# Products for z and the first gate in steps between the q, k, v blocks, and weights loaded as half tiles

## The chip, the core and the metric

The kernel runs on one core of one Trainium2 chip. Five engines matter here: TensorE (PE in the profile, PEld for its weight loads), VectorE (DVE), ScalarE (ACT), GpSimd (POOL) and SyncE (SP, which issues most of the transfers). Each runs its own queue of instructions in a fixed order, and they wait for each other through semaphores. The metric is the device time of one execution in microseconds.

## The reference

One residual block over 256 tokens of 2048 channels, in fp32. Only its first part, the token mixers, is touched by the change:

```python
def hybrid_mixer(h, w_in, conv_qkv, a_log, dt_bias, gdn_norm, pool_w, pool_scale,
                 w_branch_a, w_branch_b, w_mix_out):
    qkv, z, b_raw, a_raw, p, gate_a, gate_b = jnp.split(h @ w_in, splits, axis=-1)
    qkv = jax.nn.silu(causal_dwconv(qkv, conv_qkv))
    q, k, v = jnp.split(qkv, [QK_W, 2 * QK_W], axis=-1)      # 16 heads of 128
    ...
    o = gated_delta_rule(q, k, v, g, beta)
    o = rms_norm(o, gdn_norm) * jax.nn.silu(z.reshape(B, S, GDN_HEADS, GDN_DV))
    y_a = o.reshape(B, S, V_W) @ w_branch_a
    y_b = multi_scale_pool(p, pool_w, pool_scale) @ w_branch_b
    merged = jax.nn.sigmoid(gate_a) * y_a + jax.nn.sigmoid(gate_b) * y_b
    return merged @ w_mix_out
```

`gated_delta_rule` works in chunks: per head it needs products of k with k and q, decays between positions, a triangular solve and a few products with the state. Behind the mixers follow a cross-attention (weights xk, xq, xv, xo) and a gated MLP (ua, ub, dn).

## The kernel before

Every fp32 weight is split in two parts of 12 bits, `whi` (cast on ACT, L154) and `wlo` (subtraction on DVE, L155), and so is each activation; a product takes three of the four partial products. Weights come from memory as `raw` tiles of 128 x 2048 (1024 KB, three buffers, L140 and L141) and are split in two halves of 1024 columns; `whi` and `wlo` have three buffers each. Both halves of a raw tile are split in one go, before the first matmul on them (`wchunk`).

There are two forms of dense product. `proj_cm` (L163) gives 128 channels by 256 tokens: 16 pairs of a matmul with `whi` over 512 columns (L171) and one with `wlo` over 256 (L174). q, k, v of a head, the beta and decay logits (ba) and the pooling input (p) take this form. `proj_tm` (L186) gives tokens by 512 channels for both token tiles; each half of weights holds two rows of 128 and makes 2 x 6 matmuls of 512 columns (L195 to L197). z, the two gates (ga, gb) and all other products take it. Each `proj` has its own PSUM buffers out of four (`ps_acc`, L75).

Small work is written as generators in two lanes, "a" and "b", and `tick()` (L126) advances each lane by one step, every four rows in `proj_cm` and after each token tile of a half in `proj_tm`. So the text of the program puts the small instructions between the pieces of the dense products. The list scheduler of the tile framework then fixes each engine's queue from this program order and from what it expects to be ready.

The 16 heads run in four groups (`gdn_group`, L534). A group is 12 blocks (q, k, v of four heads); `conv_silu` (L520) follows each: the copy `t` of one half of PSUM on ACT and the sum on DVE, the multiplication with the row factors R, the first tap `ca` on ACT, three taps on DVE, and a SiLU on ACT into KQ or `vc`. Lane "a" transposes the results (`kqT` with its squares and `ktok`, `vT` with the copy into V). Then come z of the group (L584) with a SiLU on each token tile, `drain("a")`, and `gdn_rest` (L593) is put in lane "b". Behind the group the gate ga of the same index follows (`sigm`, L857), during which lane "b" works off the beginning of `gdn_rest`: `sse` and `rinv` (DVE, POOL), eight scalings of V (VZ, L611), eight products `Ur` each on POOL and ACT (L622, L625), the matmuls `gap` (L629), Exp (L633), a mask on POOL, the matmuls `kq` (L641). The rest of `gdn_rest` goes on during the next group. In group 0 lane "b" also holds `decays`, a long chain of elementwise work on POOL, which ends with the transposes bgT (L504). After group 3 and ga come gb (four products) and p.

ACT holds one table of functions at a time: a SiLU, a sigmoid and an Exp each need their own, and an `ACT_TABLE_LOAD` stands in its queue at each switch.

Of the kernel before, what the change touches and what calls it, by code (L numbers as in the profile page):

```python
# [11 lines left out]
ALU = mybir.AluOpType  # L12
# [13 lines left out]
def kernel(  # L26
    ctx: ExitStack,
    tc: tile.TileContext,
    x: bass.AP,          # [256, 2048]
    x_cm: bass.AP,       # [2, 128, 8, 256]  x, channel-major  # L30
    mem_cm: bass.AP,     # [2, 128, 8, 256]
    w_cm: bass.AP,       # [57, 128, 2048]   (q,k,v per head; b/a; p), channel-major blocks
    w_z: bass.AP,        # [4, 128, 16, 512]
    w_ga: bass.AP,       # [4, 128, 16, 512]
    w_gb: bass.AP,       # [4, 128, 16, 512]
    w_ya: bass.AP,       # [4, 128, 16, 512]
    w_yb: bass.AP,       # [4, 128, 8, 512]
    w_mo: bass.AP,       # [4, 128, 16, 512]
    w_pool: bass.AP,     # [128, 2048]       (c | group, out block, in block, d)
    w_xq: bass.AP,       # [16, 128, 2048]  # L40
    w_xk: bass.AP,       # [16, 128, 2048]
    w_xv: bass.AP,       # [4, 128, 16, 512]
    w_xo: bass.AP,       # [4, 128, 16, 512]
    w_up: bass.AP,       # [86, 128, 2048]
    w_dn: bass.AP,       # [4, 128, 43, 512]
    conv_w: bass.AP,     # [128, 48, 4]
    ffn_w: bass.AP,      # [128, 86, 3]
    ffn_b: bass.AP,      # [128, 86]
    pregain: bass.AP,    # [128, 4, 16]      (mix, xa, mem, ffn)
    postgain: bass.AP,   # [3, 128, 2048]  # L50
    gdn_gain: bass.AP,   # [128, 1]
    pool_sc: bass.AP,    # [128, 8]
    ab: bass.AP,         # [16, 2]           (a_log, dt_bias)
    c_ident: bass.AP,    # [128, 128]
    c_le: bass.AP,       # [128, 128]        1 where partition <= column
    c_gt: bass.AP,       # [128, 128]        1 where partition > column
    c_tinit: bass.AP,    # [128, 256]
    c_invc: bass.AP,     # [128, 64]
    out: bass.AP,        # [256, 2048]
# [15 lines left out]
    def ps_acc(name):  # L75
        return acc.tile([P, 512], F32, tag="acc", name=name)
# [4 lines left out]
    # ------------------------------------------------------------ constants  # L81
# [5 lines left out]
    # x channel-major first: its products begin before the norm is known  # L87
# [27 lines left out]
    # ------------------------------------------------------------ lanes of small work,  # L115
    # emitted a step at a time between the pieces of the dense products
# [21 lines left out]
    # ------------------------------------------------------------ weights  # L138
    def wraw(src, n, name):
# [4 lines left out]
    def wchunk(src, n, name, raw=None, keep=False):  # L144
        """Load n columns of weights and split them exactly in two parts of 12 bits."""
        raw = wraw(src, n, name) if raw is None else raw
        return list(wsplit(raw, n, name, keep))

    def wsplit(raw, n, name, keep=False):
        for s in range(0, n, 1024):  # L150
            m = min(1024, n - s)
            hi = wp.tile([P, 1024], F32R, tag="whi", name=f"whi_{name}_{s}")
            lo = wp.tile([P, 1024], F32R, tag="wlo", name=f"wlo_{name}_{s}")
            pin(nc.scalar.copy(hi[:, :m], raw[:, s:s + m]), keep)  # L154
            pin(nc.vector.tensor_tensor(out=lo[:, :m], in0=raw[:, s:s + m],  # L155
                                        in1=hi[:, :m].bitcast(F32), op=ALU.subtract), keep)
            yield hi, lo, m
# [5 lines left out]
    def proj_cm(wsrc, X, name, raw=None, parts=None):  # L163
        """out^T block [128 channels, 256 tokens]: product of the high weights with
        both parts of X side by side, of the low weights with the high part."""
        ps = ps_acc(f"cm_{name}")
        kt = 0
        for hi, lo, m in parts or wchunk(wsrc, 2048, name, raw):
            for j in range(m // P):
                xk = X(kt)  # L170
                nc.tensor.matmul(ps, lhsT=hi[:, j * P:(j + 1) * P],  # L171
                                 rhs=xk.rearrange("p a s -> p (a s)"),
                                 start=(kt == 0), stop=False)
                nc.tensor.matmul(ps[:, 0:S], lhsT=lo[:, j * P:(j + 1) * P],  # L174
                                 rhs=xk[:, 0, :], start=False, stop=(kt == 15))
                kt += 1
                if kt % 4 == 0:
                    tick()
        return ps
# [6 lines left out]
    def proj_tm(wsrc, X, KT, name, tail=0, mid=None):  # L186
        """out [128 tokens, 512] for both token tiles; over the last 2 * tail rows of
        128 the first token tile goes first, and mid(its product) follows it."""
        ps = [ps_acc(f"tm{t}_{name}") for t in range(NT)]
# [9 lines left out]
        def chunks(k0, k1):  # L199
            for c0 in range(k0, k1, 4):  # L200
                n = min(4, k1 - c0)
                src = wsrc[:, c0:c0 + n, :].rearrange("p k c -> p (k c)")
                kt = c0
                for hi, lo, m in wchunk(src, n * 512, f"{name}_{c0}"):
                    yield [(kt + j, hi[:, j * 512:(j + 1) * 512], lo[:, j * 512:(j + 1) * 512])
                           for j in range(m // 512)]
                    kt += m // 512

        K0 = KT - 2 * tail
        for part in chunks(0, K0):  # L210
            for t in range(NT):
                for args in part:
                    mm(t, *args)
                tick()
        if tail:
            parts = list(chunks(K0, KT))
            for t in range(NT):
                for part in parts:
                    for args in part:
# [4 lines left out]
        return ps  # L224

    # ------------------------------------------------------------ activations
# [11 lines left out]
    def transpose_in(dst, src, gain, name):  # L238
        """src(t) [128 tokens, 512] -> dst [128, 4, 2, 256] with the gain of each channel."""
# [20 lines left out]
    def rstd_of(parts, name, tag="rstd", bufs=8):  # L260
        """(sum of the columns / 2048 + eps) ** -0.5; parts: [128, n] sums of squares."""
# [11 lines left out]
    def square_sum(src, dst, name):  # L273
        """dst [128, 1] = sum of src ** 2 over [128, 512]."""
# [3 lines left out]
    def pre_norm(src, gi, name, tiles, ss):  # L278
        """src: two [128, 2048] tiles, scaled in place; appends the transposed tiles."""
# [13 lines left out]
    def row_factors(ss, name, first=False):  # L293
        """[128, 256]: on each partition the factors of the tokens."""
# [15 lines left out]
    def cm_squares(src, name, keep=False):  # L310
        """The sums of squares of the tokens, from channel-major tiles."""
# [23 lines left out]
    def result(gen):  # L335
        while True:
            try:
                next(gen)
            except StopIteration as e:
                return e.value  # L340

# [4 lines left out]
    def norm_cm(src, R, gi, name, tiles):  # L346
        """src: channel-major tiles, normalised in place and split."""
# [57 lines left out]
    # ============================================================ 1. mixers  # L405
    raw_q = wp.tile([P, 2048], F32, tag="raw", name="raw_q0")
# [4 lines left out]
    def load_q(q):  # L411
        sl = slice(q * 1024, (q + 1) * 1024)
        nc.sync.dma_start(raw_q[:, sl], w_cm[0][:, sl])
# [7 lines left out]
    # without the factor of each token, for the first blocks  # L421
    uT = []
    qparts = []
    qsplit = wsplit(raw_q, 2048, "q0", True)
    for b in range(4):
# [9 lines left out]
        if b % 2 == 0:  # L435
            qparts.append(next(qsplit))
    raw_k = wraw(w_cm[1], 2048, "k0")
    conv_sb = cload("conv_sb", conv_w, [P, 48, 4], nc.sync)
    raw_v = wraw(w_cm[2], 2048, "v0")
    raw_ba = wraw(w_cm[48], 2048, "ba")  # L440
# [14 lines left out]
    # beta and the log decays, channel-major: b in rows 0..15, a in rows 32..47  # L455
# [3 lines left out]
    # eG[:, 0, c, h] = exp(G_i), eG[:, 1, c, h] = exp(G_last - G_i)  # L459
# [5 lines left out]
    def decays(ps):  # L465
# [17 lines left out]
        # log(1 + e) = 2 atanh(e / (2 + e))  # L483
# [50 lines left out]
    def gdn_group(gi):  # L534
# [30 lines left out]

        for hl in range(4):
            h = 4 * gi + hl
            n = f"{g_}_{hl}"
            if h == 1:
                lanes["b"].append(decays(proj_cm(w_cm[48], U0, "ba", raw_ba)))  # L570
# [628 lines left out]
```

## Time and profile before

| what | value |
|---|---|
| time, median of 3 runs | 2026.81 us (2026.27 to 2026.9) |
| span of the profiled execution | 2026.0 us |
| PE busy | 2001.8 us, 99% of the span |
| DVE busy | 1386.6 us, 68% |
| ACT busy | 1099.6 us, 54% |
| POOL busy | 108.5 us, 5% |
| ACT table loads | 19, at 1.283 us |

The profiled execution has a time of its own, the span, from the first to the last instruction; the time of a run has a little around it. Busy shares are means over the whole program. The group stage, which the change touches, runs from the start to some 580 us: four groups of about 111 us (12 blocks, z and ga), then gb and p. A matmul's row overlaps the next one's by its fill, so the distance of two starts tells what one costs.

### The profile page before, as it was taken

The numbers are of one execution on the slowest core, as the hardware profiler recorded it, in microseconds if no ns is written. First come the engines' busy times: TensorE is split into PE (matmuls) and PEld (weight loads), VectorE is DVE, ScalarE is ACT, GpSimd is POOL, SyncE is SP. The second block draws the span as 40 slices with busy tenths as digits, with TensorE's granted clock in tenths as the row PEclk, the third lists the DMA queues.
The fourth block names the chain that finished last, engine by engine and source line by source line (L and its number), as shares of the span: only waits on it lengthen the run. The fifth ranks groups of instructions, "written<-read, shape, count | busy, mean of one in ns | idle before, by whom it ended". The sixth has DMA issues, their size and how long they took to land.

```text
span 2026.0 us, 27927 instructions
## 1 busy us (share of the span) xinstructions
PE 2001.8 (99%) x10842; PEld 1703.1 (84%) x10842; DVE 1386.6 (68%) x2171; ACT 1099.6 (54%) x1826; POOL 108.5 (5%) x154
## 2 busy tenths in 40 slices
PE   8999999999999999999999999999999999999998
PEld 6888888888878888888888888788888888888886
DVE  7869687697756855678555554688888887854444
ACT  7657666566654544456444444565555555544443
POOL 1510200201100000001000000100000000000000
PEclk9999999999999999999999999999999999999999
DMA  6445354444444656456555455555555555565553
GB/s 242 166 167 183 132 184 147 160 173 146 166 170 153 236 193 249 173 199 228 185 190 175 159 207 190 204 209 187 190 189 192 193 193 187 187 231 200 188 196 141
DMA packets 55029, 377.87 MB, mean 187 GB/s; under 512 B 6768, under 2 KB 7536, under 8 KB 10224
## 3 DMA queue, kind: packets, MB, share of 16 engines
q1 hardware_dynamic: 52128, 359.73, 51.0%
q0 software_dynamic: 2192, 15.73, 2.0%
q8 instruction: 85, 1.39, 0.3%
q10 hardware_dynamic: 576, 0.62, 0.1%
q14 instruction: 48, 0.39, 0.1%
HBM read 369.77 MB, written 6.29 MB: 186 GB/s over the span
## 4 chain that ended last, share of the span: by engine, by line
PE 95%; DVE 1%; POOL 0%; ACT 0%; issue 0%; DVEq 0%; POOLq 0%; ACTq 0%
PE cm_ub L171 8%; PE cm_ua L171 8%; PE cm_ub L174 4%; PE cm_ua L174 4%; PE tm_dn L197 4%; PE tm_dn L196 4%; PE tm_dn L195 4%; PE cm_xk L171 3%; PE cm_xq L171 3%; PE cm_vg L171 3%; PE cm_kg L171 2%; PE cm_qg L171 2%; PE tm_gb L195 2%; PE cm_xk L174 1%; PE cm_xq L174 1%; PE tm_gb L196 1%
## 5 line engine op out<-in xcount | busy, mean ns | idle before, releaser
L171 PE MATMUL cm_ua<-h3T,whi_ua 128*128 128x512 f32 x688 | 242.0, 395 | 0.0
L171 PE MATMUL cm_ub<-h3T,whi_ub 128*128 128x512 f32 x688 | 241.0, 394 | 0.0
L174 PE MATMUL cm_ua<-h3T,wlo_ua 128*128 128x256 f32 x688 | 191.0, 278 | 0.0
L174 PE MATMUL cm_ub<-h3T,wlo_ub 128*128 128x256 f32 x688 | 190.7, 277 | 0.1
L155 DVE TENSOR_TENSOR wlo_dn<-raw_dn,whi_dn 128x1024 fp32r<-128x1024 f32 (+1 forms) x88 | 105.6, 1200 | 119.0 <-ACT whi_dn L154 118.8
L154 ACT CAST whi_dn<-raw_dn 128x1024 fp32r<-128x1024 f32 (+1 forms) x88 | 91.1, 1035 | 136.9 <-PE tm_dn L197 132.2
L171 PEld LDWEIGHTS cm_ua<-h3T,whi_ua 128*128 128x128 f32 x688 | 129.3, 188 | 29.8 <-ACT h3T L253 0.2
L171 PEld LDWEIGHTS cm_ub<-h3T,whi_ub 128*128 128x128 f32 x688 | 129.1, 188 | 29.9
L155 DVE TENSOR_TENSOR wlo_ub<-raw_ub,whi_ub 128x1024 fp32r<-128x1024 f32 x86 | 105.3, 1225 | 58.1 <-ACT whi_ub L154 58.0
L154 ACT CAST whi_ub<-raw_ub 128x1024 fp32r<-128x1024 f32 x86 | 90.4, 1051 | 100.3 <-issue 51.5
L154 ACT CAST whi_ua<-raw_ua 128x1024 fp32r<-128x1024 f32 x86 | 90.6, 1053 | 99.2 <-PE cm_ub L171 47.5
L195 PE MATMUL tm_dn<-whi_dn,gT 128*128 128x512 f32 x344 | 133.8, 389 | 0.0
L196 PE MATMUL tm_dn<-wlo_dn,gT 128*128 128x512 f32 x344 | 133.8, 389 | 0.0
L197 PE MATMUL tm_dn<-whi_dn,gT 128*128 128x512 f32 x344 | 133.8, 389 | 0.0
L174 PEld LDWEIGHTS cm_ub<-h3T,wlo_ub 128*128 128x128 f32 x688 | 129.2, 188 | 0.4 <-DVE wlo_ub L155 0.4
L174 PEld LDWEIGHTS cm_ua<-h3T,wlo_ua 128*128 128x128 f32 x688 | 129.5, 188 | 0.0
L155 DVE TENSOR_TENSOR wlo_ua<-raw_ua,whi_ua 128x1024 fp32r<-128x1024 f32 x86 | 105.3, 1225 | 26.6 <-ACT whi_ua L154 26.5
L171 PE MATMUL cm_vg<-uT,whi_vg 128*128 128x512 f32 x256 | 95.1, 409 | 0.0
L171 PE MATMUL cm_kg<-uT,whi_kg 128*128 128x512 f32 x256 | 93.7, 406 | 0.0
L171 PE MATMUL cm_xk<-meT,whi_xk 128*128 128x512 f32 x256 | 89.7, 396 | 0.0
L171 PE MATMUL cm_xq<-h2T,whi_xq 128*128 128x512 f32 x256 | 88.8, 394 | 0.0
L171 PE MATMUL cm_qg<-uT,whi_qg 128*128 128x512 f32 x240 | 86.4, 401 | 0.0
(412 smaller groups left out, 5350.2 us busy)
## 6 DMA issues: line engine op xcount, KB each, us to landing
raw_ua<-in_w_up_dram SPq DMA_DIRECT2D x43, 1024.0 KB, 4.8
raw_ub<-in_w_up_dram SPq DMA_DIRECT2D x43, 1024.0 KB, 4.8
raw_dn<-in_w_dn_dram SPq DMA_DIRECT2D x40, 1024.0 KB, 4.7
raw_zg<-in_w_z_dram SPq DMA_DIRECT2D x16, 1024.0 KB, 4.8
raw_ga<-in_w_ga_dram SPq DMA_DIRECT2D x16, 1024.0 KB, 4.8
raw_gb<-in_w_gb_dram SPq DMA_DIRECT2D x16, 1024.0 KB, 4.7
raw_ya<-in_w_ya_dram SPq DMA_DIRECT2D x16, 1024.0 KB, 4.8
raw_mo<-in_w_mo_dram SPq DMA_DIRECT2D x16, 1024.0 KB, 4.7
```

The source lines that it names most:

```text
L154: pin(nc.scalar.copy(hi[:, :m], raw[:, s:s + m]), keep)
L155: pin(nc.vector.tensor_tensor(out=lo[:, :m], in0=raw[:, s:s + m], in1=hi[:, :m].bitcast(F32), op=ALU.subtract), keep)
L171: nc.tensor.matmul(ps, lhsT=hi[:, j * P:(j + 1) * P], rhs=xk.rearrange("p a s -> p (a s)"), start=(kt == 0), stop=False)
L174: nc.tensor.matmul(ps[:, 0:S], lhsT=lo[:, j * P:(j + 1) * P], rhs=xk[:, 0, :], start=False, stop=(kt == 15))
L195: nc.tensor.matmul(ps[t], lhsT=xh, rhs=wh, start=(k == 0), stop=False)
L196: nc.tensor.matmul(ps[t], lhsT=xh, rhs=wl, start=False, stop=False)
L197: nc.tensor.matmul(ps[t], lhsT=xl, rhs=wh, start=False, stop=(k == KT - 1))
```

## The change

Raw tiles become half as large (1024 columns, 512 KB) and twice as many (six), and a half is split right before its first matmul. The four PSUM buffers become two pairs; the blocks of a group use pair A, z and ga pair B. z and ga of a group become one generator of 18 turns (`gdn_side`: eight halves of z, the SiLU, eight halves of ga, the gate), and `blk` runs one or two turns of it after each block, in group 0 after all but the first head's, so that the generator is at its end with the last v. `gdn_rest` is put in lane "b" at the end of the group, and the next group's q block (after group 3: gb) follows at once. The ba weights are no longer loaded ahead. Comments are stripped, so line numbers move by up to 30.

```diff
+    def ps_acc(name, pair=None):
+        if pair is None:
+            pair = "AB"[acc_n[0] // 2 % 2]
+            acc_n[0] += 1
+        return acc.tile([P, 512], F32, tag=f"acc{pair}", bufs=2, name=name)
...
-        raw = wp.tile([P, 2048], F32, tag="raw", name=f"raw_{name}")
-        nc.sync.dma_start(raw[:, :n], src)
+        raw = wp.tile([P, 1024], F32, tag="raw", bufs=6, name=f"raw_{name}")
+        nc.sync.dma_start(raw[:, :src.shape[1]], src)
...
+    def proj_cm(wsrc, X, name, raws=None, parts=None, pair=None):
+        ps = ps_acc(f"cm_{name}", pair)
+        if parts is None and raws is None:
+            raws = wraws(wsrc, name)
+        for kt in range(16):
+            if kt % 8 == 0:
+                hi, lo = parts[kt // 8] if parts else wsplit(raws[kt // 8], f"{name}_{kt}")
...
+    def tm_steps(wsrc, X, KT, name, tail=0, mid=None, pair=None):
...
+        for k in range(0, K0, 2):
+            p = part(k, min(k + 2, K0))
             for t in range(NT):
-                for args in part:
+                for args in p:
                     mm(t, *args)
                 tick()
+            yield
...
+        side = gdn_side(gi, g_, zs)
+        turn = [0, 0]
+        N = 9 if gi == 0 else 12
+
+        def blk(*args):
+            ps = proj_cm(*args, pair="A")
+            turn[0] += 1
+            while turn[1] * N < 18 * turn[0]:
+                next(side, None)
+                turn[1] += 1
+            return ps
...
-            psq = proj_cm(w_cm[3 * h], U0, f"q{n}", parts=qparts if h == 0 else None)
-            psk = proj_cm(w_cm[3 * h + 1], U0, f"k{n}", raw_k if h == 0 else None)
+                psq = blk(w_cm[3 * h], U0, f"q{n}")
+                psk = blk(w_cm[3 * h + 1], U0, f"k{n}")
...
-        ps = proj_tm(w_z[gi], U0, 16, f"z{g_}")
-        for t in range(NT):
-            nc.scalar.activation(zs[:, t, :], ps[t], AF.Silu,
-                                 scale=R0[1][t][:, 0:1])
+        for _ in side:
+            pass
         if gi == 0:
             drain("b")
         drain("a")
         lanes["b"].append(gdn_rest(gi, g_, KQ, V, zs, ktok, ss))
 
+    def gdn_side(gi, g_, zs):
+        ps = yield from tm_steps(w_z[gi], U0, 16, f"z{g_}", pair="B")
+        for t in range(NT):
+            nc.scalar.activation(zs[:, t, :], ps[t], AF.Silu,
+                                 scale=R0[1][t][:, 0:1])
+        yield
+        ps = yield from tm_steps(w_ga[gi], U0, 16, f"ga{gi}", pair="B")
+        gate(ps, mga[gi // 2][:, gi % 2])
...
     for gi in range(4):
-        gdn_group(gi)
         if gi % 2 == 0:
             mga.append(b8(f"mga{gi}").rearrange("p (n t s) -> p n t s", n=2, t=2))
-        sigm(w_ga[gi], mga[gi // 2][:, gi % 2], f"ga{gi}")
+        gdn_group(gi)
```

The order of the instructions at the end of group 1 shows what moves. In the rows a name carries its group and head (`vc_g1_3` is the fourth v of group 1, `whi_qg2_0_8` the second half of the first q block of group 2) and a number of its own at the end. First PE before, where the last `vT` of the group stands:

```order
L197 MATMUL tm1_zg1_2273<-whi_zg1_12_1024_2448,uT3_145 128x512
L562 MATMUL vT_g1_3_2476<-ident_82,vc_g1_3_2261 128x128 x2
L195 MATMUL tm0_ga1_2482<-whi_ga1_0_0_2486,uT0_110 128x512
L196 MATMUL tm0_ga1_2482<-wlo_ga1_0_0_2487,uT0_110 128x512
L197 MATMUL tm0_ga1_2482<-whi_ga1_0_0_2486,uT0_110 128x512
...
L629 MATMUL gap_g10_2527<-Ur_g1_2517,m_gtr_166 128x512 x2
L195 MATMUL tm1_ga1_2483<-whi_ga1_0_0_2486,uT0_110 128x512
```

The whole of z stands between the last v block and its transposes, and ga around what follows. The same place on PE now:

```order
L180 MATMUL cm_vg1_3_2627<-uT3_146,wlo_vg1_3_8_2653 128x256
L554 MATMUL kqT_g1_3_2685<-ident_82,KQ_g1_1331 128x128 x4
L178 MATMUL cm_qg2_0_2708<-uT0_111,whi_qg2_0_0_2713 128x512
...
L567 MATMUL vT_g1_3_2699<-ident_82,vc_g1_3_2674 128x128 x2
L661 MATMUL gap_g10_2752<-Ur_g1_2742,m_gtr_169 128x512 x2
L661 MATMUL gap_g11_2785<-Ur_g1_2742,m_gtr_169 128x512
L673 MATMUL kq_g10_2812<-KQ_g1_1331 128x256
L178 MATMUL cm_qg2_0_2708<-uT2_133,whi_qg2_0_8_2765 128x512
```

Only the first half of the next q block (16 matmuls) and `kqT` stand between the last v block and `vT`. On ACT, the queue at that place before:

```order
L154 CAST whi_ga1_0_1024_2490<-raw_ga1_0_2484 128x1024
L625 ACTIVATE Ur_g1_2517<-m_le_162,g_lo_182 128x128 x2
L586 ACTIVATE VZ_g1_1377<-tm0_zg1_2272,rstd_h0_285 128x512
L625 ACTIVATE Ur_g1_2517<-m_le_162,g_lo_182 128x128 x3
L563 COPY VZ_g1_1377<-vT_g1_3_2476 128x256
L586 ACTIVATE VZ_g1_1377<-tm1_zg1_2273,rstd_h1_291 128x512
L611 ACTIVATE VZ_g1_1377<-VZ_g1_1377,rinv_g1_2502 128x128 x2
L154 CAST whi_ga1_4_0_2565<-raw_ga1_4_2563 128x1024
L633 ACT_TABLE_LOAD
L633 ACTIVATE UD_g1_2518<-gap_g10_2527 128x512
L154 CAST whi_ga1_4_1024_2569<-raw_ga1_4_2563 128x1024
L633 ACTIVATE UD_g1_2518<-gap_g11_2552 128x512
```

A cast stands after every few small instructions, and there is one table load. The queue of ACT at that place now, from the sixth scaling on:

```order
L530 ACTIVATE ca_vg1_3_2679<-xp0_95,conv_sb_159 128x256
L643 ACTIVATE VZ_g1_1332<-VZ_g1_1332,rinv_g1_2727 128x128 x5
L657 ACTIVATE Ur_g1_2742<-m_le_165,g_lo_185 128x128
L537 ACT_TABLE_LOAD
L537 ACTIVATE vc_g1_3_2674<-ca_vg1_3_2679 128x256
L657 ACTIVATE Ur_g1_2742<-m_le_165,g_lo_185 128x128
L158 CAST whi_qg2_0_8_2765<-raw_qg2_0_1024_2711 128x1024
L568 COPY VZ_g1_1332<-vT_g1_3_2699 128x256
L665 ACT_TABLE_LOAD
L665 ACTIVATE UD_g1_2743<-gap_g10_2752 128x512
L643 ACTIVATE VZ_g1_1332<-VZ_g1_1332,rinv_g1_2727 128x128 x2
L657 ACTIVATE Ur_g1_2742<-m_le_165,g_lo_185 128x128 x4
```

Two table loads and the SiLU of `vc` now stand among the scalings, and one cast in this stretch; the next, `whi_zg2_0`, follows the last row.

## Rows read from the trace of the kernel before

**Rows 1.** Engine shares of the page: busy time, share of the span, instructions.

```profile
PE 2001.8 (99%) x10842; PEld 1703.1 (84%) x10842; DVE 1386.6 (68%) x2171; ACT 1099.6 (54%) x1826; POOL 108.5 (5%) x154
```

**Rows 2.** Waits of PE: for what, us in total, times, longest.

```profile
PE cm_qg L171 <- ACT whi_q L154: 8.4, 1, 8.4
PE bgT L504 <- POOL st L499: 1.7, 1, 1.7
PE cm_vg L174 <- DVE wlo_vg L155: 1.3, 1, 1.3
```

**Rows 3.** 50 us windows: PE, PEld, DVE, ACT, POOL busy, clock, DMA share, GB/s.

```profile
100.00:150.00 50.00, 50.00 (x230) 41.53 (x229) 30.30 (x57) 29.67 (x49) 5.77 (x6) 1.00 0.49 170
400.00:450.00 50.00, 50.00 (x276) 43.11 (x275) 46.92 (x115) 31.58 (x53) 2.88 (x3) 1.00 0.50 171
```

**Rows 4.** Windows of 3.41 us behind the bgT wait, same columns.

```profile
72.85:76.26 3.41, 3.41 (x14) 3.02 (x14) 2.24 (x5) 1.73 (x4) 0.00 (x0) 0.50 0.66 274
76.26:79.67 3.41, 3.41 (x21) 3.04 (x21) 3.04 (x6) 2.68 (x6) 2.47 (x4) 1.00 0.36 86
```

**Rows 5.** Groups of ACT, 85 to 125 us: count, busy us, mean ns, idle before.

```profile
L154 ACT CAST whi_zg<-raw_zg 128x1024 fp32r<-128x1024 f32 x8 | 8.4, 1048 | 8.2 <-PE tm_zg L197 4.1 <-PE cm_vg L171 2.2 <-issue 1.2
L532 ACT ACTIVATE vc_g<-ca_vg 128x256 f32<-128x256 f32 x2 | 0.8, 410 | 0.0
L525 ACT ACTIVATE ca_vg<-xp,conv_sb 128x256 f32<-128x256 f32 x1 | 0.5, 507 | 0.0
```

**Rows 6.** The same of DVE.

```profile
L155 DVE TENSOR_TENSOR wlo_zg<-raw_zg,whi_zg 128x1024 fp32r<-128x1024 f32 x8 | 9.8, 1224 | 8.1 <-ACT whi_zg L154 8.1
```

**Rows 7.** DMA issues: count, KB each, median us to landing.

```profile
raw_zg<-in_w_z_dram SPq DMA_DIRECT2D x16, 1024.0 KB, 4.8
raw_pool<-in_w_pool_dram SPq DMA_DIRECT2D x2, 512.0 KB, 3.7
```

**Rows 8.** Timeline of PE: start, us, line, out<-in.

```profile
93.91 0.40 PE L171 MATMUL cm_vg<-uT,whi_vg 128*128 128x512 f32 x1
94.27 0.40 PE L171 MATMUL cm_vg<-uT,whi_vg 128*128 128x512 f32 x1
...
116.15 0.38 PE L562 MATMUL vT_g<-ident,vc_g 128*128 128x128 f32 x2
116.28 0.48 PE L195 MATMUL tm_zg<-whi_zg,uT 128*128 128x512 f32 x1
...
119.12 0.39 PE L195 MATMUL tm_ga<-whi_ga,uT 128*128 128x512 f32 x1
...
126.82 1.02 PE L641 MATMUL kq_g<-KQ_g 128*128 128x256 f32 x4
127.50 0.58 PE L195 MATMUL tm_ga<-whi_ga,uT 128*128 128x512 f32 x1
```

**Rows 9.** Timeline of POOL, end of the chain of decays.

```profile
71.78 0.53 POOL L499 TENSOR_SCALAR st<-st,aexp 16x256 f32<-16x256 f32 x1
```

**Rows 10.** Timeline of ACT, 103 to 123 us.

```profile
103.38 0.42 ACT L532 ACTIVATE vc_g<-ca_vg 128x256 f32<-128x256 f32 x1
...
108.71 0.27 ACT L554 ACTIVATE j_g<-kqT_g 128x128 f32<-128x128 f32 x1
...
109.72 0.28 ACT L556 COPY ktok_g<-kqT_g 128x128 f32<-128x128 f32 x1
111.94 0.99 ACT L611 ACTIVATE VZ_g<-VZ_g,rinv_g 128x128 f32<-128x128 f32 x3 [1.94 <-POOL rinv_g L603]
...
119.90 1.04 ACT L154 CAST whi_ga<-raw_ga 128x1024 fp32r<-128x1024 f32 x1
120.96 1.28 ACT L633 ACT_TABLE_LOAD   x1
122.25 0.60 ACT L633 ACTIVATE UD_g<-gap_g 128x512 f32<-128x512 f32 x1
122.75 1.04 ACT L154 CAST whi_ga<-raw_ga 128x1024 fp32r<-128x1024 f32 x1
```

More of the change, by code (lines that the diff above doesn't have):

```diff
@@ L136, in drain, with wraw, wraws, wsplit @@
             step(lanes[k])
-    def wraw(src, n, name):
-        raw = wp.tile([P, 2048], F32, tag="raw", name=f"raw_{name}")
-        nc.sync.dma_start(raw[:, :n], src)
-        return raw
[L144 to L157, printed above, removed]
+    def wraw(src, name):
+        raw = wp.tile([P, 1024], F32, tag="raw", bufs=6, name=f"raw_{name}")
+        nc.sync.dma_start(raw[:, :src.shape[1]], src)
+        return raw
+    def wraws(src, name):
+        return [wraw(src[:, s:s + 1024], f"{name}_{s}") for s in range(0, src.shape[1], 1024)]
+    def wsplit(raw, name, n=1024, keep=False):
+        hi = wp.tile([P, 1024], F32R, tag="whi", name=f"whi_{name}")
+        lo = wp.tile([P, 1024], F32R, tag="wlo", name=f"wlo_{name}")
+        pin(nc.scalar.copy(hi[:, :n], raw[:, :n]), keep)
+        pin(nc.vector.tensor_tensor(out=lo[:, :n], in0=raw[:, :n],
+                                    in1=hi[:, :n].bitcast(F32), op=ALU.subtract), keep)
+        return hi, lo
     def pin(ins, keep=True):
@@ L161, in pin @@
             tc.keep_in_program_order(ins)
[L163 to L178, printed above, removed]
+    def proj_cm(wsrc, X, name, raws=None, parts=None, pair=None):
[5 more added lines that the diff above has]
+                hi, lo = parts[kt // 8] if parts else wsplit(raws[kt // 8], f"{name}_{kt}")
+            sl = slice(kt % 8 * P, (kt % 8 + 1) * P)
+            xk = X(kt)
+            nc.tensor.matmul(ps, lhsT=hi[:, sl], rhs=xk.rearrange("p a s -> p (a s)"),
+                             start=(kt == 0), stop=False)
+            nc.tensor.matmul(ps[:, 0:S], lhsT=lo[:, sl], rhs=xk[:, 0, :], start=False,
+                             stop=(kt == 15))
+            if kt % 4 == 3:
+                tick()
         return ps
@@ L224, in proj_tm, with result @@
         return ps
+    def result(gen):
+        while True:
+            try:
+                next(gen)
+            except StopIteration as e:
+                return e.value
+    def proj_tm(*args, **kw):
+        return result(tm_steps(*args, **kw))
     def xtile(name):
@@ L333, in cm_squares @@
         return [s2[:, t:t + 1] for t in range(NT)]
[L335 to L340, printed above, removed]
     def new_ss(name):
@@ L403, in piece @@
             return self.y[t][:, sl]
-    raw_q = wp.tile([P, 2048], F32, tag="raw", name="raw_q0")
+    raw_q = [wp.tile([P, 1024], F32, tag="raw", bufs=6, name=f"raw_q0{q}") for q in range(2)]
     def load_x(i, q):
@@ L435 @@
         if b % 2 == 0:
-            qparts.append(next(qsplit))
-    raw_k = wraw(w_cm[1], 2048, "k0")
+            qparts.append(wsplit(raw_q[b // 2], f"q0{b}", keep=True))
+    raw_k = wraws(w_cm[1], "k0")
     conv_sb = cload("conv_sb", conv_w, [P, 48, 4], nc.sync)
-    raw_v = wraw(w_cm[2], 2048, "v0")
-    raw_ba = wraw(w_cm[48], 2048, "ba")
+    raw_v = wraws(w_cm[2], "v0")
     m_le = cload("m_le", c_le, [P, P], nc.sync)
```

50 lines of the change are left out of this document (24 added, 26 removed).

## Prediction

> **What bounds the kernel now.** I read the shares of the engines first, then what TensorE (PE) waited for, then 50 us windows over the stage that the change touches, then the timelines at the end of one group. PE is busy 2001.8 of 2026.0 us, ScalarE (ACT) 54% of the span [rows 1]. The longest wait of PE, 8.4 us, is the start of the program, which the change leaves as it is [rows 2]. In the stage of the four groups the nine windows from 100 to 550 us all show PE busy 50.00 of 50; two stand here, and they leave 18 to 20 us of each free on ACT and 3 to 20 on VectorE (DVE) [rows 3]. What this stage can still give back is the wait for bgT (1.7 us) and one for a low half (1.3) [rows 2], and a stretch of half clock: right behind the bgT idle the granted clock was 0.50 for 3.41 us with 14 matmuls in it, and 1.00 in the next 3.41 us with 21 [rows 4], so between 3.41 x 7/21 = 1.1 and 3.41/2 = 1.7 us went there. That is at most 5 us, 0.25%. So the question is hardly what the change wins, but whether PE stays fed.
>
> PE is fed by a chain: the transfer of a half of weights, its cast on ACT (1.05 us) [rows 5], its subtraction on DVE (1.22 us) [rows 6], with three halves of run-ahead; all engines run their queues in a fixed order. A late instruction on ACT delays every cast behind it.
>
> **The change part by part.** *Same work.* Matmuls, casts and subtractions keep their numbers and shapes. From the gb products on only the small work of the last group moves; what follows, two thirds of the time, I cost at 0.
>
> *Half tiles.* A half now has its own transfer of 512 KB and six buffers; before, two halves shared one of 1024 KB in three: the same store. 1024 KB land in 4.8 us, 512 KB in 3.7 [rows 7]. A half is used up in 2.7 us (12 matmuls from 116.28 to 119.12, less 0.1 for the transposes ahead) [rows 8]; with six in flight there is 3.7 us of transfer against some 16 us of lead: 0. Only with one in flight at a time would it cost 3.7 - 2.7 = 1.0 us a half, and nothing forces that.
>
> *PSUM in pairs.* A q, k or v block has two buffers and not four, so the third block waits for the copy and sum of the first, about 0.4 us each at vc's shape [rows 5]. A step of z or ga, 2.7 us at the least, lies between: 0.
>
> *The bgT wait.* On ACT the new order puts one more table load (1.28) and a SiLU between the sigmoid and the exponential ahead of POOL's chain of polynomials, whose last link ended at 72.31 [rows 9]; so the chain starts about 1 us later, and on PE the bgT transposes come 0.6 us of work earlier. The wait grows from 1.7 to some 3.3: +1.6. Bounds: -1.7 (it vanishes) and +3. The small waits in front of it are swallowed by it: 0.
>
> *The ends of the groups.* This term decides. Before, PE had the eight halves of z behind the last v of a group, and then eight of ga: the last vc was ready at 103.8 us [rows 10] and its transposes came only at 116.15 [rows 8]; the squares, scalings and decays of gdn_rest lay beside some 40 us of dense products, whose casts need 1.05 of each 2.7 us of ACT. After, z and ga are used up when the last v ends, and the last vc and the start of gdn_rest stand in ACT's and PE's queues between the very next weights. I count ACT from the end of the last v of group 1 in the new order (PSUM copies at vc's 0.41 [rows 5]; scalings and the Ur, which have one shape, at 0.33; squares with ktok 1.29, from 108.71 to 110.00 [rows 10]). Rest of a cast 0.5, copy t 0.41, one Ur 0.33, squares and ktok 1.29: 2.5. Then ACT stands still for sse and rinv, 1.94 as before [rows 10]: 4.5. A scaling 0.33, ca 0.51, five scalings 1.65, Ur 0.33, table load 1.28, SiLU vc 0.41, Ur 0.33: 9.3. Only now comes the second half of the next q block: 10.4, its low half at 11.6. Copy of V 0.41, table load 1.28, Exp 0.60, two scalings and four Ur 1.98, cast whi_zg_0 1.05: 15.7; its low half 1.22: 16.9.
>
> PE's work up to the first use of that low half: kqT 0.4 (four transposes, at half of what two vT take, 0.2), the q block 16 x 0.36 = 5.7, vT 0.2, four gap matmuls at 0.225 = 0.9, three heads of kq at 0.85 (0.68 to the next start, 1.02 to the end) = 2.6, two z matmuls 0.46 [rows 8]: 10.3. PE loses 16.9 - 10.3 = 6.6; as ACT's short instructions overlap (the Exp at 122.25 ran 0.60, the next cast began at 122.75), I take 6.1. First PE sits at vT (3.3 us of work stand ahead of it, vc comes at 9.0), then at the low half of q, then at the one of z. The ends of groups 2 and 3 read the same, with gb for q after group 3: 3 x 6.1 = 18.3. At the end of group 0 the last step of ga follows v, and both q halves are cast by then: ACT goes t 0.41, table load, two sigmoids (at Exp's 0.60; the second waits for PE's 2.7): 3.3; ca, squares, ktok, two Ur: 5.8; table load, SiLU, eight scalings, copy of V, four Ur: 11.8; table load, Exp, two Ur, cast, subtraction: 16.6. PE has 2.7 + 0.4 + 5.7 + 0.2 + 0.9 + 3.4 + 0.46 = 13.8. Loss 2.8.
>
> Bounds of one end: 0, if a run-ahead of three halves (8.1 us) covers it; 9, if the heads of kq don't fill the waits.
>
> *Clock.* After 1.7 us of idle the clock was halved for 3.41 us, at a price of 1.1 to 1.7 [rows 4]. Each of the four ends has a stall as long; but part of a halved stretch will fall in the next wait. 1.0 each: 4.0, between 0 and 13.6 (two such stretches at each end, 1.7 apiece).
>
> *Table loads.* The order has 31 on ACT where it had 19. Those at the ends are in the sum above; the others, like the rest of the 12 x 1.28 = 15.4 us, have room in ACT's free time [rows 3]. In the trace a load starts right behind a cast (119.90 + 1.04; load at 120.96) and Exp follows at 122.25, so a switch costs 1.3 us [rows 10]. The Trainium skill (ScalarE: Activation LUTs, What ACT_TABLE_LOAD costs and Rules for kernel authors) speaks against this change: it advises to do all of one table set before switching, and gives about 2.7 us for a switch, load and drain together. The trace shows the load and no drain behind a cast; by the page's figure the nine loads at the ends would add some 1.4 each, an estimate of 12 us more, and the time would be 2066.
>
> Sum: 2.8 + 18.3 + 4.0 + 1.6 = 26.7. The profiled execution spans 2026.0 us, the runs took 2026.3 to 2026.9, median 2026.8, so 0.8 lies around the span: 2026.0 + 26.7 + 0.8 = 2053.5. **Forecast: 2054 us, 1.3% slower.**
>
> **Rivals.** *Half hidden.* If ACT doesn't stand still for rinv at the ends (1.94 each) and the Ur there, which wait for nothing late, have run before v ends (seven x 0.33 = 2.3), each end loses about 2, and the clock less: 2026.8 + 4 x 2 + 2 = 2037. For it: ACT has 18 us of 50 free ahead of the end [rows 3]. Against: in the new order the Ur stand behind the squares, and a queue passes nothing.
>
> *No stall, and the bgT wait won.* It decides at the end of a group: if the run-ahead of three halves (8.1) is longer than what ACT does ahead of the second q half (10.4), PE never waits; that is short by 2.3 only. If PE then also comes to bgT after POOL's chain, 1.7 and the half clock of 1.1 to 1.7 come back, and 2026.8 - 3.2 = 2023.6, at best 2021.5 with the low half's wait. For it: ACT's free time again. Against: vT stands in PE's order ahead of the second q half, and its vc comes at 9.0.
>
> *Deeper.* PE works the 10 to 14 us of each end at half clock for the most part, since one stall follows the other: 4 x 5 in place of 4.0, so 2070; with 9 lost at each end 2080. Against: the one halved stretch in the groups lasted 3.41 us [rows 4].
>
> That the products are not interleaved after all is excluded by the order.
>
> **How the numbers follow.** Forecast 0.62 (2040 to 2068), half hidden 0.14 (2031 to 2040), no stall 0.13 (2021 to 2031), deeper 0.11 (2068 to 2085). Since the trace has no drain, 0.02 of the forecast's 0.62 is for the page's dearer switch, within the same bounds. What can be told from no change is 0.2%, 4 us: of the no-stall case 0.04 lies below 2022.8 and 0.09 within; the rest, 0.87, is slower. The range leaves out about a tenth on either side: 2029 to 2072.
>
> **What would show it.** Right: the 50 us windows that hold the ends of groups (near 138, 250, 360 and 475 us) fall to 43 to 48 of PE, with clock under 1.00; PE waits there at vT, whi_qg, wlo_qg, wlo_zg and wlo_gb, 2 to 5 us at a time; bgT waits 3 us; ACT has 15 us more; the time from gb on is that of before. Wrong: PE stays at 50.00 in these windows; waits for raw tiles appear behind the casts (then the half tiles matter); or the waits are spread over all blocks and not gathered at the four ends (PSUM pairs, or late casts everywhere).

## The result, and the profile after

The changed kernel took 2061.2 us (2059.65 to 2062.12) against 2026.7: 34.5 us more, a ratio of 1.0167 with a 95% interval of 1.0154 to 1.018. The forecast was 2054, slower. The span of the profiled execution is 2060.4 us against 2026.0.

Where the time went is bounded first by a tile that both kernels have behind the touched stage, the products ya with the branch weights. The row of after gives number, duration in ns (least, median, most), first and last start:

```profile
L201 PE MATMUL tm_ya<-whi_ya,oT_g x128: 387/389/476, 722.8 to 848.4; 128*128 128x512 f32 x128
```

The first ya matmul starts at 722.8; in the kernel before it was 688.7. So 34.1 of the 34.4 us are lost in the mixers, and the rest of the program runs as before. Two windows, of before and then of after, split them (columns of [rows 3]):

```profile
0.00:688.70 688.70, 675.90 (x3962) 572.17 (x3963) 508.34 (x973) 428.76 (x856) 86.52 (x115) 1.00 0.49 169
0.00:722.80 722.80, 689.59 (x3963) 578.13 (x3964) 510.16 (x973) 444.87 (x868) 92.74 (x115) 0.98 0.54 163
```

For the same matmuls PE stood idle 20.4 us longer (33.2 for 12.8) and was busy 13.7 us longer. The engine shares of after, and its waits of PE of a us or more in the mixers, but for the one at the start of the program (7.9, before 8.4), in the columns of [rows 1, 2]:

```profile
PE 2015.5 (98%) x10842; PEld 1708.8 (83%) x10842; DVE 1388.9 (67%) x2171; ACT 1115.0 (54%) x1838; POOL 114.7 (6%) x154
```

```profile
PE vT_g L567 <- ACT vc_g L537: 10.5, 3, 4.0
PE bgT L509 <- POOL st L504: 4.6, 1, 4.6
PE cm_qg L178 <- ACT whi_qg L158: 2.4, 2, 1.2
PE kq_g L673 <- ACT UD_g L665: 2.0, 1, 2.0
PE cm_qg L180 <- DVE wlo_qg L159: 1.5, 2, 0.8
PE tm_zg L201 <- ACT whi_zg L158: 1.3, 1, 1.3
PE tm_gb L202 <- DVE wlo_gb L159: 1.2, 2, 0.8
PE tm_gb L201 <- ACT whi_gb L158: 1.2, 1, 1.2
```

The bgT wait of [rows 2] has grown from 1.7 to 4.6 us, and the other rows are new. The vT, qg, kq, whi_gb and one of the wlo_gb waits lie at the ends of groups, as these 50 us windows show (columns of [rows 3]):

```profile
150.00:200.00 50.00, 47.96 (x235) 39.85 (x234) 42.20 (x104) 32.12 (x59) 3.18 (x4) 0.97 0.53 159
250.00:300.00 50.00, 44.15 (x235) 37.47 (x234) 30.55 (x63) 34.85 (x82) 14.17 (x14) 0.93 0.36 105
400.00:450.00 50.00, 45.44 (x227) 38.00 (x226) 30.98 (x59) 34.27 (x70) 13.15 (x13) 0.93 0.43 133
550.00:600.00 50.00, 44.10 (x196) 35.87 (x195) 31.18 (x64) 36.34 (x64) 11.49 (x13) 0.93 0.45 137
```

The window from 100 to 150 us, which holds no end, is as full as in [rows 3] (PE busy 50.00, clock 1.00); those that hold an end of a group lost 2 to 6 us of PE's 50, and their granted clock is 0.93 to 0.97. The waits at the ends begin near 152, 280, 420 and 560 us. That is later than the prediction's 138, 250, 360 and 475: a group of the kernel before takes 131.5 us and not the 111 given ahead of the prediction (the q blocks of groups 1, 2 and 3 start at 145.4, 277.0 and 408.5), and what was given as the end of the stage, some 580 us, is 688.7. The stretches of half clock one by one, in the same columns (the first is at bgT, the others at the ends of groups 0, 1, 2, 2 and 3):

```profile
72.52:79.35 6.83, 6.46 (x18) 5.27 (x19) 1.90 (x4) 2.77 (x4) 5.56 (x9) 0.50 0.01 4
154.44:157.85 3.41, 3.41 (x8) 2.75 (x9) 2.33 (x5) 2.37 (x5) 0.91 (x2) 0.50 0.00 0
287.56:294.39 6.83, 5.48 (x15) 4.47 (x15) 1.93 (x3) 6.79 (x14) 0.64 (x1) 0.50 0.25 77
424.09:427.50 3.41, 2.94 (x10) 2.14 (x8) 1.46 (x4) 2.20 (x8) 2.08 (x2) 0.50 0.41 136
430.92:434.33 3.41, 3.41 (x10) 2.72 (x9) 1.75 (x3) 3.38 (x8) 0.64 (x1) 0.50 0.34 83
567.45:574.28 6.83, 4.97 (x14) 4.05 (x14) 1.57 (x3) 6.77 (x14) 1.63 (x3) 0.50 0.22 57
```

These are the answer to [rows 4], where there was one stretch of 3.41 us. I estimate that the work done in a halved stretch would have taken half as long (the pairs of q's matmuls start 0.64 us apart from 424.27 on, and 0.35 just before). PE's busy time in the five at the ends is 20.2 us, so some 10.1 went there; at bgT 3.2, where before had 1.7.

One end, that of group 1, first on ACT (start, us, line; idle time before in brackets) and then on PE:

```profile
273.65 1.28 ACT L881 ACT_TABLE_LOAD   x1
...
276.23 1.28 ACT L537 ACT_TABLE_LOAD   x1
...
277.96 1.28 ACT L881 ACT_TABLE_LOAD   x1
...
279.84 1.03 ACT L158 CAST whi_qg<-raw_qg 128x1024 fp32r<-128x1024 f32 x1
...
284.57 0.40 ACT L643 ACTIVATE VZ_g<-VZ_g,rinv_g 128x128 f32<-128x128 f32 x1 [1.64 <-POOL rinv_g L635]
...
287.15 1.28 ACT L537 ACT_TABLE_LOAD   x1
288.44 0.42 ACT L537 ACTIVATE vc_g<-ca_vg 128x256 f32<-128x256 f32 x1
...
289.06 1.03 ACT L158 CAST whi_qg<-raw_qg 128x1024 fp32r<-128x1024 f32 x1
...
293.91 1.03 ACT L158 CAST whi_zg<-raw_zg 128x1024 fp32r<-128x1024 f32 x1
```

```profile
280.92 0.50 PE L178 MATMUL cm_qg<-uT,whi_qg 128*128 128x512 f32 x1 [1.19 <-ACT whi_qg L158]
...
282.18 0.39 PE L180 MATMUL cm_qg<-uT,wlo_qg 128*128 128x256 f32 x1 [0.76 <-DVE wlo_qg L159]
...
288.91 0.69 PE L567 MATMUL vT_g<-ident,vc_g 128*128 128x128 f32 x2 [3.90 <-ACT vc_g L537]
```

The last v block of the group ended near 279.2 (the transposes kqT, 0.60 long, start at 279.14). Three table loads stand ahead of the cast of the next q's first half, which ends at 280.87; PE waits 1.19 for it and 0.76 for its low half. Then come the squares, the idle time for rinv (1.64, in [rows 10] 1.94), the scalings, a load, and the SiLU of vc, which ends at 288.86, 9.6 us behind the v block; PE waits 3.90. The second q half and whi_zg follow at 290.1 and 294.9, 10.9 and 15.7 behind the block.

The table loads on ACT by line, SiLU of q, k, v and sigmoid of the gates:

```profile
L537 ACT ACT_TABLE_LOAD x13 | 16.7, 1283 | 0.2
L881 ACT ACT_TABLE_LOAD x8 | 10.3, 1283 | 0.1
```

They were 5 and 4 before; in all 31 against 19.

### The profile page after: what moved, and what is told of

Read it like the earlier page. It is cut to its first block, busy times and chain, and to the rows that moved or that the text cites. A ratio compares the mean times of both kernels' runs of the same rounds, so it can differ in the third digit from the quotient of the medians.

```text
span 2060.4 us, 28816 instructions
## 1 busy us (share of the span) xinstructions
PE 2015.5 (98%) x10842; PEld 1708.8 (83%) x10842; DVE 1388.9 (67%) x2171; ACT 1115.0 (54%) x1838; POOL 114.7 (6%) x154
## 4 chain that ended last, share of the span: by engine, by line
PE 90%; ACT 2%; DVE 1%; POOL 1%; issue 1%; DVEq 0%; POOLq 0%; ACTq 0%
PE cm_ub L178 8%; PE cm_ua L178 8%; PE cm_ub L180 4%; PE tm_dn L201 4%; PE tm_dn L203 4%; PE tm_dn L202 4%; PE cm_ua L180 4%; PE cm_xk L178 3%; PE cm_xq L178 3%; PE cm_qg L178 2%; PE cm_vg L178 2%; PE cm_kg L178 2%; PE cm_xk L180 1%; PE cm_xq L180 1%; PE tm_xv L201 1%; PE tm_xv L202 1%
```

## The experiments

Each kernel ran on the same chip as the kernel before, in rounds; ratios are to that. The kernel before took 2026.7 to 2027.4 us in these sets, so times from different sets compare to about 1 us. In the cuts of edits `...` stands for lines left out. Names e1 to e6, f1, f5 and g1 to g4 stand for the labels.

**e1: no steps.** z and the gate in one piece again, everything else of the change kept.

```diff
-            while turn[1] * N < 18 * turn[0]:
-                next(side, None)
-                turn[1] += 1
...
-        for _ in side:
-            pass
+        for _ in range(9):
+            next(side)
...
         lanes["b"].append(gdn_rest(gi, g_, KQ, V, zs, ktok, ss))
+        for _ in side:
+            pass
```

> The changed kernel with z in one piece behind the last v of a group and the first gate behind that, as before; half tiles, the split of each half right before its use, and the PSUM pairs stay. Theory (the ends of the groups, where the start of the small work of a group stands between the casts of the next weights, and the half clock behind these waits): 2027 us, within 3 of the kernel before, no wait of PE at vT, whi_qg or wlo_zg, 20 table loads. Rival (smaller transfers, late split or PSUM pairs slow the feed): 2040 or more, with waits for raw, spread over all blocks.

Measured: 2032.9 us, ratio 1.0028 (1.0017 to 1.0039). The ends closed, but some 6 us stayed, where at most 3 were expected. Its new waits of PE:

```profile
PE tm_ga L201 <- ACT VZ_g L618: 2.7, 3, 0.9
PE cm_vg L178 <- DVE xp L189: 1.8, 3, 0.6
```

The gate waits until z's SiLU has freed pair B, a v block until q's sum has freed pair A. That is a term I had put at 0. f5 tests it.

**f5: e1 with the four PSUM buffers in one rotation.** The `pair` arguments of the calls go too.

```diff
-        return acc.tile([P, 512], F32, tag=f"acc{pair}", bufs=2, name=name)
+        return acc.tile([P, 512], F32, tag="acc", name=name)
```

> The kernel of e1 (no steps, half tiles, late split) with the four PSUM buffers in one rotation again. In e1 PE waited 0.9 us at the start of the gate for z's SiLU and 0.6 us at a v block for the sum of q, three times each. Theory (these waits are the pairs'): both gone, 4.5 us less than e1, 2028 us (2026.5 to 2030). Rival (half tiles and the late split cost the rest, the pairs nothing): 2032 to 2034.

Measured: 2027.1 us, ratio 0.9998 (0.9989 to 1.0007). The pairs made the 5.8 us of e1, and half tiles with the late split cost nothing that can be measured. What they do cost is covered: the packets of the weights' queue took 58.0% of the time of the 16 transfer engines, in the kernel before 51.0% for the same bytes.

In the changed kernel itself neither of e1's two waits appears: there a step of z or ga lies between the blocks, as the prediction had it.

**e2: both halves of a block split ahead.**

```diff
+            if kt == 0 and not parts:
+                parts = [wsplit(raws[i], f"{name}_{8 * i}") for i in range(2)]
             if kt % 8 == 0:
-                hi, lo = parts[kt // 8] if parts else wsplit(raws[kt // 8], f"{name}_{kt}")
+                hi, lo = parts[kt // 8]
```

> The changed kernel, but both halves of a q, k or v block are cast and split ahead of its first matmul. Theory: the second q half no longer stands behind vc, but vc still comes some 9.4 us behind the last v where PE has 6.1 us of work, and the cast of whi_zg_0 is as late as before: each of the last three ends loses about 5 in place of 6, in all 2056 us (2051 to 2061). Rival (the late split of single halves is the cause): the ends close, 2035 or less.

Measured: 2056.1 us, ratio 1.0143 (1.0126 to 1.016), on the number, though not by its terms. The late split is not the cause; it is worth 5 us. PE waits less at vT and more behind it, and its idle time up to the first ya is only 1.7 us less than in the changed kernel (31.5 for 33.2). The rest is the clock: the halved stretches of the mixers hold 14.1 us of PE's work where the changed kernel has 26.7, some 6.3 us less by half. The three ends were to lose about 5 each; the idle time is 4.4, 2.8 and 5.9.

```profile
PE vT_g L569 <- ACT vc_g L539: 6.3, 5, 3.9
PE kq_g L675 <- ACT UD_g L667: 3.7, 3, 2.0
```

**e3: only z in steps.** `18 *` becomes `9 *` in the loop of `blk`, and the gate runs behind `lanes["b"].append(...)` as in e1.

> The changed kernel with only z in steps between the blocks; the first gate follows the group in one piece, with the start of the small work beside it. Theory: eight halves of the gate, 22 us of work for PE, cover the 17 us that ACT needs at an end: no wait there, 2031 us (2027 to 2036), what is left being the wait for bgT and the half clock behind it. Rival (steps between the blocks cost as such, by late casts or table loads inside the group): half of the loss stays, 2044.

Measured: 2037.6 us, ratio 1.0052 (1.0037 to 1.0067): halfway between the two, and outside the range of the theory. The waits of PE:

```profile
PE vT_g L567 <- ACT vc_g L537: 6.4, 4, 1.6
PE bgT L509 <- POOL st L504: 5.0, 1, 5.0
```

Eight halves cover all but vT: vc is late by 1.6 us at each of four ends, where before it had z behind it. With 3.3 more at bgT that makes 9.7 us. The half clock at bgT lasts 6.83 us for 3.41, but 2.9 of it lie in the wait, so its price is some 2.0 for 1.7; smaller waits ahead of bgT became 1.1 less. That is 8.9 of the 9.7 between the spans (2035.7 for 2026.0), so steps of z cost at most about a us by themselves; what z gave to vT before was overlooked.

**e4: the lane of transposes not emptied.** `tok` is set behind the copy of the last vT, and the second cut leaves out yields of the substitution.

```diff
-        drain("a")
-        lanes["b"].append(gdn_rest(gi, g_, KQ, V, zs, ktok, ss))
+        def later():
+            while not tok:
+                yield
+            yield from gdn_rest(gi, g_, KQ, V, zs, ktok, ss)
+        lanes["b"].append(later())
...
-            if r > 6 or r in (2, 4, 6):
+            if r > 18 or r in (2, 4, 6, 7, 9, 11, 13, 15, 17):
```

> The changed kernel with all its steps, but at the end of a group the lane of transposes is not emptied, and the small work of the group begins only when the last vT has come by its own ticks, four to six steps into the next group (six of the yields in the substitution are left out, so that it ends in time). 29 table loads, as good as the 31 of the changed kernel. Theory: the casts of the next q block and of z stand ahead of the small work, so the ends close: 2033 us (2028 to 2040) with the bgT wait left. Rival (the added table loads are the cause, wherever they stand): 2055 or more.

Measured: 2050.9 us, ratio 1.0117 (1.0102 to 1.0132): a miss, and nearer to the rival. vT no longer waits, but:

```profile
PE p_g L749 <- ACT TM_g L736: 3.5, 4, 1.3
PE cm_qg L178 <- ACT whi_qg L158: 3.2, 2, 1.7
```

The wait for whi_qg is still there, 3.2 us for 2.4, and at the end of group 1 the three table loads, which this edit leaves, still stand ahead of that cast (274.10, 276.68 and 278.41; the cast starts at 280.29). PE also waits at p_g, by the shortened substitution or by its later start; no run separates the two. So the small work behind the last v was not the whole of it, and the loads got a test of their own.

**f1: gates stored raw.** `AF.Sigmoid` becomes `AF.Identity` in `gate`: this kernel leaves the sigmoid of the gates out, and with it 16 of the 31 table loads.

> The changed kernel with the sigmoid of the gates left out (the scaled products are stored raw), so that 16 of the 31 table loads are gone; the planner then puts the casts of the next q block and of z ahead of the small work at the end of a group. First theory (the small work itself stands between the casts, 14 us of ACT; the loads are 2.6 us of it): each end still loses 3 to 4, 2045 us (2041 to 2051). Second theory, now its rival (the loads around the two sigmoids, which hold ACT before the last v ends, make it late and make the planner put the casts behind): only vT waits, some 1.4 us at each of three ends with the clock unharmed, and bgT as before: 2036 us (2032 to 2040).

Measured: 2043.0 us, ratio 1.0074 (1.0061 to 1.0088), 18.3 us less than the changed kernel: inside the first theory's range, but by the second theory's waits. But for whi_zg's 1.3, of the waits listed above only vT and bgT are left at more than a us:

```profile
PE vT_g L567 <- ACT vc_g L537: 6.4, 4, 2.3
PE bgT L509 <- POOL st L504: 4.6, 1, 4.6
```

The waits for whi_qg, wlo_qg, whi_gb and wlo_gb are gone, and two of the three stretches of half clock that are left follow vT waits of 2.27 us, which the second theory had at 1.4 with the clock unharmed. So taking the loads away gives back over half of the loss. It also changes the order of the casts on ACT (shown under g4), and how much is the time of the loads and how much the order no run separates.

**e6 and e5: bgT later,** in the changed kernel and in the kernel before.

```diff
-        yield from wait(14)
+        yield from wait(20)
```

> The changed kernel with the same edit, wait(20) for wait(14). Theory: the wait of 4.6 us and half of the 6.8 us of half clock behind it go, 8 us: 2053 us (2051 to 2055). Rival (POOL's chain is late everywhere, or the stall moves on to the next late cast): 2057 or more.

> The kernel before with the transposes of bgT six ticks later in the program (wait(20) for wait(14)). Theory: the wait of 1.7 us and the stretch of half clock behind it, 1.1 to 1.7, go: 2023.5 us (ratio 0.9984). Rival (another wait takes its place, or the clock falls anyhow): 2025 to 2027.

Measured: e6 2053.9 us, ratio 1.0128 (1.0114 to 1.0142), 7.3 less than the changed kernel. e6 is as expected. e5 2024.65 us, ratio 0.9986 (0.9977 to 0.9995), where 0.9984 was expected: a little faster than the kernel before. In e5 the place of [rows 4] has full PE and full clock:

```profile
70.00:80.00 10.00, 10.00 (x60) 8.60 (x59) 9.79 (x15) 6.04 (x11) 1.91 (x2) 1.00 0.62 211
```

**g1: the gate's sigmoid behind gb.** The steps store the gate raw; bgT is six ticks later.

```diff
         gate(proj_tm(w_gb[nb], U0, 16, f"gb{nb}"), mgb[nb // 2][:, nb % 2])
+        nc.scalar.activation(mga[nb // 2][:, nb % 2], mga[nb // 2][:, nb % 2], AF.Sigmoid)
```

> All steps of the changed kernel, but a gate is stored raw in its step and its sigmoid comes in place behind each gb product, where that table is loaded anyway; and bgT six ticks later. 24 table loads, none of a sigmoid inside the groups. Theory (the loads around the sigmoids make two thirds of what the ends lose): f1's 2043 less the 7.3 us that the later bgT gave the changed kernel, 2036 us (2032 to 2040). Rival (what f1 gained came from work left out, not from the table): 2050, as with bgT alone.

Measured: 2043.6 us, ratio 1.0082 (1.0067 to 1.0097): a miss of 8, and between theory and rival. ACT at the end of group 1 tells why:

```profile
269.75 1.28 ACT L893 ACT_TABLE_LOAD   x1
271.04 1.06 ACT L893 ACTIVATE mga<-mga 128x1024 f32<-128x1024 f32 x1
...
277.27 1.28 ACT L537 ACT_TABLE_LOAD   x1
```

The planner (the list scheduler) had drawn a late sigmoid of a gate (L893) forward into this place: a load, the sigmoid, and a load back for vc, 3.6 us ahead of vT, which waits 3.9 again. I had counted the loads in the order, but not where they stand.

**g4: the same, with that sigmoid pinned in program order** by `pin(...)` around it, which keeps it at its place in the text of the program.

> g1 with the late sigmoids pinned in program order, since in g1 the planner had drawn each of them forward to the end of a group (a table load 1.28, the sigmoid 1.06 and the reload ahead of vc 1.28, all before vT). 17 table loads in the order, none of them between the last v of a group and its vc. Theory: vc comes as early as in f1, vT waits 2.3, 2.3 and 1.4 at most, 2036 us (2032 to 2039). Rival (the sigmoid drawn forward is not what held vc in g1): 2042 or more, with vT waits of 3.9.

Measured: 2034.0 us, ratio 1.0036 (1.0021 to 1.005), in the range, and the waits at vT are 2.26, 2.26 and 1.37 us, as expected. All steps of the change are in it, and against e6, which has the same bgT, only the place of the gate's sigmoid differs: 19.9 us. By the traces PE's idle time up to the first ya is 11.3 us less (17.8 for 29.1), and e6's halved stretches there, with 17.3 us of PE's work in them, are gone (some 8.6). ACT's order at the end of group 1:

```profile
265.93 1.05 ACT L158 CAST whi_qg<-raw_qg 128x1024 fp32r<-128x1024 f32 x1
...
268.18 1.03 ACT L158 CAST whi_qg<-raw_qg 128x1024 fp32r<-128x1024 f32 x1
...
270.30 1.03 ACT L158 CAST whi_zg<-raw_zg 128x1024 fp32r<-128x1024 f32 x1
271.23 0.36 ACT L188 COPY t_vg<-cm_vg 128x256 f32<-128x256 f32 x1
```

Both halves of the next q and the first of z are cast ahead of the last copy t (in the changed kernel that copy starts at 280.77, and the second half of q and z are cast from 289.06 and 293.91). That settles the loads around the sigmoids, with the order that the planner makes of them, as the larger cause.

**g2: g1 and e4 together; g3: the last four halves of the gate held back to the end of the group** (`14 *` in the loop of e3, bgT later).

> g1 and e4 together: gates late, bgT later, the lane of transposes not emptied at the end of a group. Theory (with the casts of q and z ahead and no vc to wait for, nothing at the ends is late): no wait at vT, whi_qg or wlo_qg; what is left is e4's wait at p_g, 3.5 us and a stretch of half clock: 2030 us (2026 to 2034). Rival (steps between the blocks cost something by themselves): 2036 or more.

> The changed kernel with the last four halves of the gate held back to the end of the group, bgT six ticks later, and 20 table loads. Theory (an end needs PE work that is cast already; four halves are 11 us, and vc comes some 8 us behind the last v where PE has 7): waits of about 1 us at vT, clock unharmed, 2030 us (2026 to 2036). Rival (all eight are needed): 2042 or more.

Measured: g2 2037.5 us, ratio 1.0054 (1.0037 to 1.0071); g3 2037.8 us, ratio 1.0052 (1.0037 to 1.0067). Both missed by 8; g2 came out at its rival's number, g3 between its two. g3's waits at vT are 1.9 us at each end and not 1, and the clock halved behind three of them:

```profile
PE vT_g L567 <- ACT vc_g L537: 7.4, 4, 1.9
```

In g2 no vT wait is left, but p_g waits, and two casts of gb are late:

```profile
PE p_g L749 <- ACT TM_g L736: 3.6, 4, 1.4
PE tm_gb L201 <- ACT whi_gb L158: 2.5, 2, 1.3
```

The spans of g2's four runs are 2033.7 to 2037.5 at mean clocks of 0.998 and 0.996, so part of the miss is clock, in some runs and not in others. The profiled execution, at 2033.7, has no halved stretch in the mixers; against that of e5 (2023.2) PE stands idle 7.1 us longer up to the first ya (18.1 for 11.0) and is busy 2.3 us longer (676.8 for 674.5). That rest, which no wait explains, is all that steps by themselves can have cost there; whether they did stays open.

## Why the prediction was right, and where it was off

*What bounds it, and the sign.* Right. PE was full, nothing of size was to be had, and the loss is PE waiting for casts and for vc, which stand late in ACT's queue, with half clock at these waits. It lies at the four ends and at bgT, the time behind the mixers did not move, and ACT has 15.4 us more. In the total, 34.4 for 26.7, errors of the terms cancel in part: the idle time at the ends came out smaller than forecast, the clock and bgT dearer.

*The ends, by their terms.* The forecast was 2.8 + 18.3 = 21.1 us. The idle time there is 2.0 (kq, end 0), 1.19 + 0.76 + 3.90 = 5.9 (end 1), 4.6 (end 2) and 5.9 (end 3), together 18.3. For end 1 the sum had vc at 9.3 behind the last v, the second q half at 10.4 and whi_zg at 15.7; the trace has 9.6, 10.9 and 15.7. What the sum left out is the wait of 1.95 us ahead of these, for the first half of q. The waits that it put behind vT, for the low halves of q's second half and of z, did not come: from 287.56 to 294.39 PE worked at half clock, and with that work spread out the low halves seem to have been there in time. Idle time and clock are then not two terms that simply add.

*The clock* is the term that was mis-sized: 4.0, and it is some 10.1. I took one stretch of 3.41 us for each end, and let part of it fall into the next wait. There were 23.9 us of half clock at the ends, two stretches of 6.83 and three of 3.41, and 20.2 of them hold PE's work, since the work behind the waits is dense. Idle and half clock together are 28.4 at the ends, where the sum had 25.1.

*bgT.* +1.6 forecast. The wait grew by 2.9, and the stretch of half clock there doubled, some 1.5 more, which I had not counted. The transposes started 0.5 later and not 1, but PE reached the place 2.35 earlier (68.27 for 70.62). 1.2 of this is less work ahead of it, where I had 0.6; the waits ahead of it fell by the rest (two for low halves, 2.0 together, and 0.45 at the start gone, one for whi_zg, 1.3, new).

These terms make 28.4 + 2.9 + 1.5 = 32.8, less 1.2 for those small waits, and 0.5 for a new one at wlo_gb: 32.1 of the 34.1. The idle time is all in them; the other 2.0 us are in PE's busy time, 13.7 us longer, of which half clock explains some 11.6. Which instructions took them stays open.

*Table loads.* Here the reason, not the number, was incomplete. I said that the loads which are not at the ends have room in ACT's free time. Three of them stand in a row ahead of the last v's end (273.65 to 279.24), around the two sigmoids of a gate and the SiLU of a k between them, and the cast of the first q half stands behind them. f1 and g4 show more: with the sigmoids out of the groups the planner puts the casts of q and z ahead of the small work, and 18 to 20 us come back. That the small work of `gdn_rest` follows the last v at once, which I gave as the cause, is the smaller part: g4 keeps it, and loses 9.3 us against e5. The two parts do not add: moving the small work alone gave back 10.3 us (e4), and moving both (g2) is no better than g4. The Trainium skill's rule (ScalarE: Activation LUTs, Rules for kernel authors) to do all of one table set before switching is what g4 follows for the sigmoids, and its time bears the rule out. The price of some 2.7 us that these rules give for a switch is not what the trace has: load at 287.15, SiLU at 288.44, 1.29. That 2061.2 lies nearer to the 2066 that the prediction worked out from that price than to its own 2054 is luck: all 28 loads of the mixers that have an instruction ahead of them start 0.02 us behind it, and the next function follows 0.01 us behind the load's end.

*Half tiles* at 0: right (f5). *PSUM pairs* at 0: right in the changed kernel, but for the cover named; without it they cost 5.8 us (e1 against f5). *The rivals:* "half hidden" would have needed the Ur and rinv early; in f1 and g4 the planner did put all eight Ur of a group on ACT ahead of the last copy t, but ACT still stood idle 2.17 us for rinv, so that 2034 in g4 is near its 2037 by half of its condition only. "No stall" failed at vT. "Deeper" was right that half clock comes again and again, but its 20 us for it are twice what was measured. Two side sums do not follow from the prediction's own terms: the low half's wait of 1.3 takes 2023.6 to 2022.3 and not to 2021.5, and 9 lost at each of four ends would make 2084 and not 2080.

## What to carry to other kernels

Where one engine is full, a step that is moved is judged by what the other queues hold at the place it leaves: dense work behind a short dependent chain is its cover, and using it up earlier moves the chain into the open. Activation functions of different tables that come ready at the same time cost a load each, and they can also change the order that a planner makes; here it paid to keep the sigmoids out of the stage and to collect them behind it, pinned, since unpinned they were drawn back in. A wait of TensorE is to be priced with a stretch of half clock as a possibility, at its full length if the work behind the wait is dense: in the changed kernel every end had one or two, at vT waits of 2.3 us in g4 there was none.

## What the runs showed of the chip that was not expected

The length of one wait does not tell by itself whether the clock falls. In e3 waits of 1.6 us left it at 1.00; after 1.74 in the kernel before it was halved. A vT wait of 2.27 us, ended at 284.53 in f1, was followed by half clock; in g4 the same wait of 2.26 was not. The wait in g4 and a window behind it, and then the halved stretch behind that of f1:

```profile
278.51 0.44 PE L567 MATMUL vT_g<-ident,vc_g 128*128 128x128 f32 x2 [2.26 <-ACT vc_g L537]
```

```profile
278.50:282.00 3.50, 3.49 (x17) 2.95 (x18) 2.13 (x2) 3.47 (x6) 0.36 (x1) 1.00 0.43 116
```

```profile
284.67:288.08 3.41, 3.41 (x10) 2.74 (x10) 1.97 (x2) 3.38 (x7) 0.42 (x1) 0.50 0.45 119
```

In f5 the clock fell from 25.57 to 28.98 us with no wait longer than 0.3 in the 3 us before; what PE did there was sixteen matmuls of one column each, 1.87 us of its busy time. In the kernel before the same sixteen left the clock at 1.00. In the changed kernel the three longest waits in the mixers, 4.62, 3.95 and 3.90, each had 6.83 us of half clock, which began 0.4 to 1.9 us before the wait ended. And the same bytes in transfers of half the size took 58.0% of the time of the 16 transfer engines for 51.0%, at no cost in time here (f5).
